# One block of a matrix product transposed by DMA instead of on TensorE, its first group reordered, and its block loads split in two and chained

## Chip, core and metric

The kernel runs on one core of one Trainium2 chip. The metric is the device time of one execution in microseconds; the figure for the kernel before is the median of three runs. Engines are called by their names: TensorE (PE in the views; PEld is its weight load), VectorE (DVE), ScalarE (ACT), GpSimd (POOL) and SyncE (SP). GpSimd issues the loads here, SyncE the stores and the DMA transposes.

## What is computed

```python
m, k, n = 2048, 2048, 2048          # a: m x k, b: k x n, gamma: n, all float32
x = np.matmul(a, b)
rms = np.sqrt(np.mean(x ** 2, axis=-1, keepdims=True) + eps)
return (gamma * x / rms).astype(np.float32)
```

## The kernel before, in words

**Blocks, groups, halves.** `a` is cut into 16 blocks of 128 rows (blocks 0 to 15), the output columns into two halves of 1024 (j = 0, 1), each half into two chunks of 512. Two blocks make a group g (blocks 2g and 2g + 1). The kernel keeps all of `b` in SBUF as bf16 (`raw`), loaded once. A matmul takes a 128 x 128 piece of transposed `a` as weights and a 128 x 512 piece of `b` as the moving operand and sums into one of eight PSUM banks: `tbank` and `acc[0]` to `acc[6]`.

**Head (blocks 0 to 3).** While `b` arrives, blocks 0 to 3 are multiplied plainly for the left half, and blocks 0 and 1 for the right half (`head_matmul`, L456, called by `stream_right`, L526). From there on every pair of blocks is multiplied for each half by seven products instead of eight (Strassen's scheme in Winograd's form): four quarters of `a` (2 blocks by even and odd pieces of k) and four of `b`. `product_matmul` (L359) issues one of the 8 matmuls of one of the products 1 to 7. Products 1, 2 take quarters of block 2g, 4 takes a quarter of block 2g + 1, and 5, 6, 7, 3 take sums of quarters, sum 1, 2, 3 and 4, which VectorE computes in `a_sums` (L337) from both transposed blocks. `PAIR` is group 1 (blocks 2 and 3), whose right half is done in this form while the head ends: banks `u2` = `acc[4]`, `u4` = `acc[5]`, `p7` = `acc[6]`. Its four chunks are `x11`, `x12`, `x21`, `x22`, and `plain` names the four chunks of blocks 0 and 1 on the right.

**Groups 2 to 7.** `halves` numbers the remaining (group, half) pairs: n = 0 is group 2 left, n = 1 group 2 right, n = 2 group 3 left, and so on. `do(n, m)` (L624) issues product m of half n and the copy by ScalarE that must follow it: after product 1, bank b1 is copied to bank b2; products 2 and 6 then go on summing in b1 and b2; after 6, b2 is copied to b3, where 5 and 3 go on summing; 4 goes on in b2; 7 has its own bank `B7` = `acc[2]`. Banks of an even n are b1 `acc[1]`, b2 `acc[3]`, b3 `acc[6]`; of an odd n `acc[0]`, `acc[4]`, `acc[5]`. `take(n, 11/12/22/21)` (L643) brings a result chunk from its bank to its place in SBUF (ScalarE copies 11 and 12, VectorE adds 22 and 21). So a product waits for the copy or add that frees or fills its bank, and for the sum or transposed block that is its weight operand.

**Preparing a block.** `load_block(mb)` (L135) loads 128 x 2048 float32, 1 MB, in one transfer that GpSimd issues; block 8 goes into the free end of `head_at`, others take turns in two buffers. `row_norm(mb)` (L226, ScalarE, two squares of 1024 columns and a root), `row_factor` (L236) and a scaling to fp16 (VectorE) follow. Then the block is transposed. Block 4 and block 5 are transposed on TensorE: `row_apply` (L247) scales the whole block, `transpose_half` (L197) issues 8 transposes per half of the block into a PSUM bank, `take_transposed` (L207) copies the bank to `at(mb)`. From block 6 on `prepare` (L251) does it: each half is scaled, and SyncE issues a DMA transpose of that half into `at(mb)`. `wait_for(src)` (L148) makes GpSimd copy one element of `src`, so that GpSimd's next load waits until `src` is there.

**Finishing rows.** `square_half`, `take_pre`, `square_right` (L282 to L306) make a row's rms on ScalarE with small sums on VectorE; `finish(mb, order)` (L313) multiplies each half of a block by 1/rms and gamma on VectorE, and SyncE stores it. The halves of x live in eight SBUF slots which are used again: half 0's chunks of block 4 take the slot of block 0's left half once that is stored.

**Order.** The schedule is written by hand: each engine runs its instructions in the order in which the program issues them, and waits at each for its operands. The part at issue is the code between the head and `first_segment` (L566 to L613), `first_segment` (L659, half 0) and `segment` (L689, halves 1 and on). Before the change its order on TensorE is: PAIR's product 7's end, product 6, product 3, product 5; block 4's 16 transposes; six matmuls of PAIR's product 4, block 5's first 8 transposes, the last two of product 4, block 5's other 8 (`turn`, L596); then do(0,1), do(0,7), do(0,2), do(0,6), do(1,1), do(0,5), do(0,4), do(1,6), do(0,3), do(1,2), do(2,1) and on. Blocks 6, 7 and 8 are loaded as soon as their buffers are free.

Of the kernel before, what the change touches and what calls it, by code (L numbers as in the profile page):

```python
# [17 lines left out]
def kernel(  # L18
# [13 lines left out]
    nc = tc.nc  # L32
    P = 128
# [101 lines left out]
    def load_block(mb):  # L135
        if mb == HB + 4:
            a32[mb] = head_flat[:, 2 * K:].bitcast(FP32)
        else:
            a32[mb] = a_pool.tile([P, K], FP32, name="a32")
        nc.gpsimd.dma_start(out=a32[mb], in_=a[mb * P:(mb + 1) * P, :])  # L140

    def load_gamma(j):
        half = slice(j * HALF, (j + 1) * HALF)
# [380 lines left out]
    def stream_right(kp):  # L524
        first, second = ([(g, 2 * kp + t) for g in plain] for t in range(2))
        if kp == 0:  # L526
            for both in zip(first, second):
                for g, kt in both:
                    head_matmul(banks[g], *g, kt)
            product_matmul(PAIR, 1, 1, u2, kp, True)  # L530
            product_matmul(PAIR, 1, 2, u4, kp, True)
            return
        product_matmul(PAIR, 1, 1, u2, kp, True)
        for g, kt in first:
            head_matmul(banks[g], *g, kt)
        if kp == KP - 1:
            product_matmul(PAIR, 1, 7, p7, kp - 1, True)
        product_matmul(PAIR, 1, 2, u4, kp, True)
        if kp < KP - 1:
            product_matmul(PAIR, 1, 7, p7, kp - 1, True)  # L540
        for g, kt in second:
            head_matmul(banks[g], *g, kt)

    for kp in range(KP):
        load_later(1)
        b_diff(1, kp)
# [17 lines left out]

    r2, r3 = HB - 2, HB - 1
    x11, x12, x21, x22 = (x_chunk(r, c) for r in (r2, r3) for c in (2, 3))
    copy_on("A")(out=x11, in_=u2)
    product_matmul(PAIR, 1, 7, p7, KP - 1, True)  # L570
    b_rest(1, KP - 1)
    add(x11, u4, x11)
    evict(plain[:1], "A")
    row_norm(HB)
    row_norm(HB + 1)
    product(PAIR, 1, 6, u2, start=False)
    nc.vector.tensor_copy(out=u4, in_=u2)
    row_factor(HB)
    row_apply(HB)
    evict(plain[1:2], "D")  # L580
    row_factor(HB + 1)
    row_apply(HB + 1)
    evict(plain[2:3], "A")
    product(PAIR, 1, 3, acc[0])
    product(PAIR, 1, 5, u4, start=False)
    turned = [transpose_half(HB, h, (tbank, acc[1])[h]) for h in range(2)]
    take_transposed(HB, 0, turned[0], nc.scalar.copy)
    take_transposed(HB, 1, turned[1], nc.vector.tensor_copy)
    load_block(HB + 3)
    for r in range(HB):  # L590
        take_pre(r)
    square_right(0)
    evict(plain[3:], "A")
    square_right(1)

    def turn(h):  # L596
        view = transpose_half(HB + 1, h, (tbank, acc[2])[h])
        take_transposed(HB + 1, h, view, nc.vector.tensor_copy)

    for kp in range(KP):  # L600
        if kp == 6:
            turn(0)
        product_matmul(PAIR, 1, 4, u2, kp, False)
    turn(1)
    load_block(HB + 4)
    a_sums(G0, (3, 1, 2), False)

    def pair_ends():
        nc.scalar.copy(out=x22, in_=p7)
        nc.scalar.copy(out=x12, in_=u4)  # L610
        add(x21, u2, x22)
        add(x22, x12, x22)
        add(x12, acc[0], x12)  # L613

    halves = [(g, j) for g in range(G0, NG) for j in range(2)]
    B1, B2, B3, B7 = (acc[1], acc[0]), acc[3:5], (acc[6], acc[5]), acc[2]

    def chunks(n):  # L620
        g, j = halves[n]
# [2 lines left out]
    def do(n, m, copies=True):  # L624
# [1 line left out]
        if n >= len(halves) or n < 0:  # L626
            return
        g, j = halves[n]
        b1, b2, b3 = B1[n % 2], B2[n % 2], B3[n % 2]
# [13 lines left out]
    def take(n, what, engine="A"):  # L643

        x11, x12, x21, x22 = chunks(n)
        if what == 11:
            copy_on(engine)(out=x11, in_=B1[n % 2])
# [11 lines left out]
    def first_segment():  # L659
        n, g, j = 0, G0, 0  # L660
        nxt = 2 * g + 2
        do(n, 1)
        do(n, 7, False)
        finish(0, (1,))
        pair_ends()
        do(n, 2)
        row_norm(nxt)
        a_sums(g, (4,))
        finish(0, (0,))
        do(n, 6)  # L670
        do(n + 1, 1)
        prepare(nxt)
        do(n, 5)
        nc.scalar.copy(out=chunks(n)[2], in_=B7)
        take(n, 22)
        row_norm(nxt + 1)
        take(n, 11)
        finish(1)
        do(n, 4)
        take(n, 21)  # L680
        prepare(nxt + 1)
        square_half(2 * g + 1, j)

    X2, W2, Y2 = tbank, B1[1], B1[0]
# [5 lines left out]
    def segment(n):  # L690
# [4 lines left out]
            block_segment(n)  # L695
            return
        first = g >= G2 and (g - G2) % 2 == 0
        do(n, 6)
        own = nxt + (g == NG - 2)
        if j == 0:  # L700
            finish(ra - 1)
# [10 lines left out]
        else:  # L712
# [316 lines left out]
```

## Time and profile before

| what | value |
|---|---|
| median of 3 runs | 218.91 us (218.74 to 219.53) |
| profiled execution, its own time | 218.44 us |
| its span, first to last instruction | 216.7 us |
| mean granted TensorE clock | 0.995 |
| TensorE busy | 206.6 us (95%), 996 matmuls and transposes |
| VectorE / ScalarE / GpSimd busy | 169.3 (78%) / 114.4 (53%) / 34.5 us (16%) |
| DMA | 46.60 MB, mean 215 GB/s |
| loads of blocks 6, 7, 8 issued at | 63.29, 66.17, 66.94 us |
| ... and landed after | 5.1, 6.1, 8.0 us |
| a DMA transpose of half a block, issue to landing | 3.0 / 3.3 / 5.7 us (least, median, most) |
| a store of half a block of rows, the first four | 2.6 / 2.8 / 4.8 us |

The profiled execution is one execution, and all durations of single instructions come from it. A timeline line has its start and length in us, engine, line of the kernel, operation and tiles; an instruction may start before the one ahead of it on its engine has quite ended, since they are pipelined. Matmuls follow one another every 0.216 us, while each is drawn 0.38 us long. A line of waits has the waiting engine, its tile and line, whom it waited for, and the total, the count and the longest.

### The profile page before, as it was taken

To read this page: it belongs to the slowest core of one execution; us is meant where nothing else is said; L and a number is where in the kernel's file an instruction comes from. 1 tells how busy PE (TensorE), PEld (TensorE's weight loads), DVE (VectorE), ACT (ScalarE), POOL (GpSimd) and SP (SyncE) were. 2 spreads that over 40 slices of the span, in tenths; PEclk is the share of its full clock that TensorE was granted. 3 is DMA by queue.
4 is the path that set the end of the run, shared out by engine and by line. 5 is a ranking of instruction groups with operands and counts; after the bars stand their busy time and mean duration, and the time that the engine had idled before them with its cause. 6 is when DMAs were issued, how large, how long until landed. Compare 5 with 4: busy or idle time off the path is not lost.

```text
span 216.7 us, 2965 instructions
## 1 busy us (share of the span) xinstructions
PE 206.6 (95%) x996; PEld 96.8 (45%) x1016; DVE 169.3 (78%) x336; ACT 114.4 (53%) x226; POOL 34.5 (16%) x73
## 2 busy tenths in 40 slices
PE   7999999999999999999999999999999999999960
PEld 3544544444455444444444444444444444444420
DVE  1127869999999997789875899479868999587981
ACT  2110001810499579499635972495686834556661
POOL 7554444433001000100021001101010000000010
PEclk9999999999999999999999999999999999999998
DMA  6999999999959788988574985588995971031446
GB/s 149 168 203 206 203 204 210 209 211 210 399 213 366 306 241 239 288 327 238 180 225 162 360 265 97 194 221 266 262 297 178 287 144 58 39 122 72 197 135 252
DMA packets 37040, 46.60 MB, mean 215 GB/s; under 512 B 22561, under 2 KB 26657, under 8 KB 35745
## 3 DMA queue, kind: packets, MB, share of 16 engines
q0 software_dynamic: 10608, 23.86, 45.0%
q1 hardware_dynamic: 26144, 22.29, 34.1%
q10 hardware_dynamic: 272, 0.26, 0.3%
q8 instruction: 8, 0.13, 0.2%
q14 instruction: 8, 0.06, 0.1%
HBM read 34.60 MB, written 16.78 MB: 237 GB/s over the span
## 4 chain that ended last, share of the span: by engine, by line
PE 91%; DMA 3%; issue 1%; ACT 1%; POOL 1%; DVE 0%; ACTq 0%; POOLq 0%
PE acc L367 63%; PE acc L457 16%; DMA early<-in_a_dram 3%; PE acc L406 3%; PE acc L448 2%; PE tbank L406 2%; PE tbank L486 2%; PE tbank L188 2%; ACT a L873 1%; POOL b L118 0%; PE acc L201 0%; PE tbank L201 0%; DVE head_at L193 0%; PE tbank L448 0%; ACT sq L981 0%
## 5 line engine op out<-in xcount | busy, mean ns | idle before, releaser
L457 PE MATMUL acc<-b,head_at 128*128 128x512 bf16 x171 | 42.1, 379 | 0.3
L279 ACT ACTIVATE sq<-x 128x1024 bf16<-128x1024 f32 (+1 forms) x31 | 31.5, 1016 | 20.2 <-DVE x L104 15.6
L367 PEld LDWEIGHTS <-s 128*128 128x128 f16 (+1 forms) x280 | 27.4, 98 | 33.1 <-DVE s L344 0.3
L318 DVE SCALAR_TENSOR_TENSOR x<-x,r,gamma_sb 128x1024 f32<-128x1024 f32 x28 | 35.0, 1282 | 0.5
L367 PE MATMUL acc<-b,head_at 128*128 128x512 bf16 x134 | 33.7, 379 | 0.3
L104 DVE TENSOR_TENSOR x<-acc,x 128x512 f32<-128x512 f32 x34 | 22.7, 687 | 10.4 <-PE acc L367 4.5
L367 PEld LDWEIGHTS <-head_at 128*128 128x128 f16 (+1 forms) x192 | 18.7, 98 | 22.2
L367 PE MATMUL acc<-b,at_even 128*128 128x512 bf16 x110 | 26.0, 379 | 0.1
L457 PEld LDWEIGHTS <-head_at 128*128 128x128 bf16 x176 | 16.9, 98 | 19.4 <-issue 0.4
L230 ACT ACTIVATE sq<-a 128x1024 bf16<-128x1024 f32 x22 | 23.3, 1058 | 2.1 <-DMA a<-in_a_dram 1.7
L367 PE MATMUL acc<-b,s 128*128 128x512 bf16 x103 | 24.2, 379 | 0.1
L367 PEld LDWEIGHTS <-at_even 128*128 128x128 f16 x160 | 15.6, 98 | 18.6
L367 PE MATMUL acc<-early,s 128*128 128x512 bf16 x93 | 23.5, 379 | 0.2
L118 POOL DMA_DIRECT2D b<-in_b_dram x32 | 17.2, 541 | 19.5 <-DMA b<-in_b_dram 13.0
L367 PE MATMUL acc<-t_left,s 128*128 128x512 bf16 x77 | 18.4, 379 | 0.1
L496 ACT COPY x<-acc 128x512 f32<-128x512 f32 x7 | 4.0, 581 | 25.3 <-PE acc L457 25.3
L639 ACT COPY acc<-acc 128x512 f32<-128x512 f32 x12 | 6.9, 574 | 8.0 <-PE acc L367 7.8
L193 DVE COPY head_at<-tbank 128x1024 bf16<-128x1024 bf16 x7 | 4.8, 692 | 7.7 <-PE tbank L188 7.7
L104 DVE TENSOR_TENSOR x<-tbank,x 128x512 f32<-128x512 f32 x9 | 6.2, 691 | 4.2 <-PE tbank L486 4.1
L876 POOL TENSOR_SCALAR x<-x,r 128x512 f32<-128x512 f32 x1 | 0.7, 697 | 48.1 <-DVE r L300 48.1
L367 PE MATMUL acc<-early,head_at 128*128 128x512 bf16 x32 | 7.7, 379 | 0.1
L104 DVE TENSOR_TENSOR early<-b 128x512 bf16<-128x512 bf16 x16 | 6.8, 422 | 0.6 <-DMA b<-in_b_dram 0.3
(157 smaller groups left out, 255.3 us busy)
## 6 DMA issues: line engine op xcount, KB each, us to landing
out_dram<-x SPq DMA_DIRECT2D x29, 512.0 KB, 3.0
a<-in_a_dram POOLq DMA_DIRECT2D x9, 1024.0 KB, 6.1
b<-in_b_dram POOLq DMA_DIRECT2D x32, 256.0 KB, 10.0
a<-in_a_dram POOLq DMA_DIRECT2D x4, 512.0 KB, 9.8
early<-in_a_dram POOLq DMA_DIRECT2D x7, 256.0 KB, 10.0
gamma_sb<-in_gamma_dram POOLq DMA_DIRECT2D x2, 512.0 KB, 9.9
head_at<-in_a_dram POOLq DMA_DIRECT2D x1, 1024.0 KB, 8.0
out_dram<-x SPq DMA_DIRECT2D x3, 256.0 KB, 2.6
```

Source lines behind the costliest of these rows:

```text
L104: nc.vector.tensor_tensor(out=out, in0=in0, in1=in1, op=op)
L118: nc.gpsimd.dma_start(out=raw[j][kp][:, t, :], in_=b[lo:lo + P, j * HALF:(j + 1) * HALF])
L188: nc.tensor.matmul(view[:, t, r, :], ah(kp)[:, r, t * P:(t + 1) * P], identity, is_transpose=True, start=(t == 0 and r == 0), stop=(t == 1 ...
L193: nc.vector.tensor_copy(out=head_at[:, 2 * kp:2 * kp + 2, :, :], in_=view)
L230: nc.scalar.activation(out=junk, in_=a32[mb][:, h * HALF:(h + 1) * HALF], func=ACTF.Square, scale=2.0 ** -8, accum_out=n2[:, h:h + 1])
L279: nc.scalar.activation(out=sq[:, 0:src.shape[-1]], in_=src, func=ACTF.Square, scale=inv_sqrt_n, accum_out=msq[mb][:, c:c + 1])
L318: nc.vector.scalar_tensor_tensor(out=x, in0=x, scalar=inverse_of[mb], in1=gamma_sb[:, h * HALF:(h + 1) * HALF], op0=ALU.mult, op1=ALU.mult)
L367: nc.tensor.matmul(bank, lhsT[:, kp, :], rhs, start=(start and kp == 0), stop=(kp == KP - 1), skip_group_check=not start)
L406: nc.tensor.matmul(bank, lhsT[:, k, :], rhs, start=(m in (1, 7) and k == 0), stop=(k == KQ - 1), skip_group_check=m not in (1, 7))
L448: nc.tensor.matmul(bank, lhsT[:, k, :], rhs[:, k, :], start=(m in (1, 7) and k == 0), stop=(k == KQ - 1), skip_group_check=m not in (1, 7))
L457: nc.tensor.matmul(bank, head_at[:, kt, r, :], head_rhs(c, kt), start=(kt == 0), stop=(kt == KT - 1))
L639: nc.scalar.copy(out=b3, in_=b2)
```

## The change

- Block 5 is scaled in two halves into `a16_first`, and SyncE transposes each by DMA; `turn` and its 16 TensorE transposes and two evictions are gone.
- Around it the order of the first group changes. x11's copy and the first four matmuls of PAIR's product 6 move ahead of the head's last four matmuls. PAIR's product 3 is cut into 4 + 2 + 2 matmuls and its product 4 into 6 + 2, and these lie between product 5, block 4's transposes and the products of group 2. Half 1's products 1 and 2 and its 6 move forward: do(0,1), do(1,1), do(0,2), do(1,2), the end of product 3, do(0,7), do(0,6), product 6 of half 1, do(0,5), do(0,4), do(0,3), do(2,1). Half 1's products 1 and 2 sum in `tbank` instead of `acc[0]`.
- `prepare(6)` now stands directly behind do(0,7), ahead of `finish(0, (0,))`; `finish(1)` is cut in two; `square_right(0)` and `square_right(1)` come behind do(0,1) and do(1,1).
- `load_block` issues two transfers of 1024 columns each. Block 7's load waits until block 6 is there (its last column), block 8's until block 7 is there; the wait in `segment` goes by the last column too.

```diff
@@ load_block
-        nc.gpsimd.dma_start(out=a32[mb], in_=a[mb * P:(mb + 1) * P, :])
+        for h in range(2):
+            half = slice(h * HALF, (h + 1) * HALF)
+            nc.gpsimd.dma_start(out=a32[mb][:, half], in_=a[mb * P:(mb + 1) * P, half])
@@ stream_right
         if kp == KP - 1:
+            copy_on("A")(out=x11, in_=u2)
             product_matmul(PAIR, 1, 7, p7, kp - 1, True)
+            for k in range(4):
+                product_matmul(PAIR, 1, 6, u2, k, False)
@@ between head and first_segment
-    product(PAIR, 1, 6, u2, start=False)
+    for kp in range(4, KP):
+        product_matmul(PAIR, 1, 6, u2, kp, False)
     nc.vector.tensor_copy(out=u4, in_=u2)
     row_factor(HB)
     row_apply(HB)
     evict(plain[1:2], "D")
     row_factor(HB + 1)
-    row_apply(HB + 1)
-    evict(plain[2:3], "A")
-    product(PAIR, 1, 3, acc[0])
-    product(PAIR, 1, 5, u4, start=False)
+    def part(m, bank, lo, hi, start=False):
+        for kp in range(lo, hi):
+            product_matmul(PAIR, 1, m, bank, kp, start)
+    part(3, acc[0], 0, 4, True)
+    part(5, u4, 0, KP)
+    part(4, u2, 0, 6)
     turned = [transpose_half(HB, h, (tbank, acc[1])[h]) for h in range(2)]
     take_transposed(HB, 0, turned[0], nc.scalar.copy)
     take_transposed(HB, 1, turned[1], nc.vector.tensor_copy)
+    src, f = a32.pop(HB + 1), factor.pop(HB + 1)
+    for h in range(2):
+        half = slice(h * HALF, (h + 1) * HALF)
+        nc.vector.tensor_scalar_mul(out=a16_first[:, half], in0=src[:, half], scalar1=f)
+        nc.sync.dma_start_transpose(at(HB + 1)[:, h * KP:(h + 1) * KP, :], a16_first[:, half])
+    wait_for(a32[HB + 2][:, K - 1:K])
     load_block(HB + 3)
     for r in range(HB):
         take_pre(r)
-    square_right(0)
-    evict(plain[3:], "A")
-    square_right(1)
...
-    load_block(HB + 4)
-    a_sums(G0, (3, 1, 2), False)
...
+    part(4, u2, 6, KP)
+    part(3, acc[0], 4, 6, True)
+    nc.scalar.copy(out=x21, in_=p7)
+    nc.scalar.copy(out=x12, in_=u4)
+    evict(plain[3:], "A")
+    add(x22, x12, x21)
+    add(x21, u2, x21)
+    evict(plain[2:3], "D")
+    x12_pair = x12
+    def b1_of(n):
+        return tbank if n == 1 else B1[n % 2]
@@ first_segment
         do(n, 1)
+        square_right(0)
+        do(n + 1, 1)
+        square_right(1)
+        do(n, 2)
+        do(n + 1, 2)
+        part(3, acc[0], 6, KP, True)
+        finish(0, (1,))
+        a_sums(g, (3, 1, 2), False)
         do(n, 7, False)
-        finish(0, (1,))
-        pair_ends()
-        do(n, 2)
         row_norm(nxt)
-        a_sums(g, (4,))
+        prepare(nxt)
+        add(x12_pair, acc[0], x12_pair)
         finish(0, (0,))
         do(n, 6)
-        do(n + 1, 1)
-        prepare(nxt)
+        load_after(a32[HB + 3][:, K - 1:K], HB + 4)
+        product(g, 1, 6, B2[1], False)
         do(n, 5)
         nc.scalar.copy(out=chunks(n)[2], in_=B7)
+        finish(1, (0,))
+        a_sums(g, (4,))
         take(n, 22)
         row_norm(nxt + 1)
+        nc.scalar.copy(out=B3[1], in_=B2[1])
         take(n, 11)
-        finish(1)
+        prepare(nxt + 1)
         do(n, 4)
         take(n, 21)
-        prepare(nxt + 1)
+        finish(1, (1,))
         square_half(2 * g + 1, j)
@@ segment
-        do(n, 6)
+        if n > 1:
+            do(n, 6)
...
-        if g < G2:
+        if g < G2 and n > 1:
             do(n, 2)
             take(n, 11)
...
         do(n + 1, 1)
+        if n == 1:
+            take(n, 11)
...
-                wait_for(a32[nxt + 2][:, 0:1])
+                wait_for(a32[nxt + 2][:, K - 1:K])
```

More of the change, by code (lines that the diff above doesn't have):

```diff
@@ L542, in stream_right @@
             head_matmul(banks[g], *g, kt)
+    r2, r3 = HB - 2, HB - 1
+    x11, x12, x21, x22 = (x_chunk(r, c) for r in (r2, r3) for c in (2, 3))
     for kp in range(KP):
@@ L563 @@
     load_block(HB + 2)
-    r2, r3 = HB - 2, HB - 1
-    x11, x12, x21, x22 = (x_chunk(r, c) for r in (r2, r3) for c in (2, 3))
-    copy_on("A")(out=x11, in_=u2)
     product_matmul(PAIR, 1, 7, p7, KP - 1, True)
@@ L591 @@
         take_pre(r)
-    square_right(0)
+    part(4, u2, 6, KP)
+    part(3, acc[0], 4, 6, True)
+    nc.scalar.copy(out=x21, in_=p7)
+    nc.scalar.copy(out=x12, in_=u4)
     evict(plain[3:], "A")
-    square_right(1)
[L596 to L604, printed above, removed]
-    load_block(HB + 4)
-    a_sums(G0, (3, 1, 2), False)
[L608 to L613, printed above, removed]
+    add(x22, x12, x21)
+    add(x21, u2, x21)
+    evict(plain[2:3], "D")
+    x12_pair = x12
     halves = [(g, j) for g in range(G0, NG) for j in range(2)]
     B1, B2, B3, B7 = (acc[1], acc[0]), acc[3:5], (acc[6], acc[5]), acc[2]
+    def b1_of(n):
+        return tbank if n == 1 else B1[n % 2]
     def chunks(n):
@@ L628, in do @@
         g, j = halves[n]
-        b1, b2, b3 = B1[n % 2], B2[n % 2], B3[n % 2]
+        b1, b2, b3 = b1_of(n), B2[n % 2], B3[n % 2]
         if g >= G2:
@@ L646, in take @@
         if what == 11:
-            copy_on(engine)(out=x11, in_=B1[n % 2])
+            copy_on(engine)(out=x11, in_=b1_of(n))
         elif what == 12:
```

## The prediction, made before the changed kernel was run

> **What bounds the kernel.** I read the page first (shares and slices), then TensorE's waits, then the chain, then each engine's timeline from 55 to 120 us, the stretch that the change touches. The page has TensorE busy 95%, with every slice but the first and the last two full. A table of busy time by stage (us, then TensorE, weight loads, VectorE, ScalarE, GpSimd, clock, DMA share, GB/s) says the same of our stretch:
>
> ```profile
> 57.00:66.00 9.00, 8.95 (x60) 4.76 (x60) 8.55 (x24) 7.98 (x15) 0.53 (x1) 1.00 0.73 281
> 66.00:75.00 9.00, 8.95 (x51) 4.36 (x50) 8.44 (x15) 6.96 (x16) 1.06 (x2) 1.00 0.91 367
> 75.00:84.00 9.00, 8.95 (x43) 4.05 (x43) 8.17 (x18) 6.60 (x13) 0.00 (x0) 1.00 0.75 236
> ```
>
> TensorE does not pause, at full granted clock, while VectorE is at 91 to 95%: a second engine is almost full. TensorE's own waits are two, both in the first 12 us:
>
> ```profile
> PE acc L167 <- DVE pace L158: 1.5, 1, 1.5
> PE tbank L486 <- DVE head_at L193: 0.3, 1, 0.3
> ```
>
> So from 12 to 209 us the time is the sum of TensorE's instructions. What the change can save is TensorE work; what it can cost is a pause of TensorE. The chain (start, us, what) shows the transposes of blocks 4 and 5:
>
> ```profile
> 63.57 0.45 PE tbank L201 x8
> 64.02 0.45 PE acc L201 x8
> 64.47 1.29 PE acc L367 x6
> 65.76 0.45 PE tbank L201 x8
> 66.21 0.43 PE acc L367 x2
> 66.64 0.45 PE acc L201 x8
> ```
>
> **What goes.** Block 5's two groups of 8 transposes (65.76 and 66.64) stand in the chain with 0.45 us each: 2 x 0.45 = 0.90 us go. Nothing else leaves TensorE; every product keeps its 8 matmuls of 0.216 us (1.73 us). 0.90 us is the ceiling. VectorE loses two evictions (L208, 0.69 each) and gains one (acc[2], 0.68, from ScalarE).
>
> **What it adds, by waits.** I set each engine's instructions in the new order, from 56 to 118 us, each starting when its engine and its inputs are free, with the durations of the rows (eviction 0.57 ScalarE, 0.68 VectorE; square of a half with its readout 1.18; row_norm 2.57; row_factor 0.70; scaling a half 0.75; finish of a half 1.28; 0.04 from one engine to the next). The old order set in this way gives do(2,6) at 91.11 where the trace has 91.10, and block 7's first scaling at 82.01 where it has 82.03. The new order gives, in old clock:
>
> - x11's copy ends 56.65 as before; the moved first four matmuls of product 6, which overwrite its bank, start 56.94: 0.25 us spare. They push the last head matmuls back 4 x 0.216 = 0.86 us, so the eviction of plain[0], both row norms and block 4's scaling come 0.86 later (scaling ends 63.59). Its transposes start at 63.92 (0.28 spare); the second bank is copied out by 64.19, wanted 64.37 (0.13 spare).
> - Product 5 needs u4, VectorE's copy of 60.16 to 60.86. Eight matmuls of product 3 lay beside it; now four, ending 60.82. **Pause 0.07.**
> - do(0,1) needs block 4's second half, copied 65.02 to 65.70; the matmuls before it end 65.68. **Pause 0.06.**
> - Block 5 is scaled in halves at 65.62 and 66.40, so SP issues its two DMA transposes at 66.4 and 67.8. They replace nothing on SP before finish(0)'s store at 71.2, and land 3.3 and 3.2 us after issue in quiet rows: 71.1. The first left operand made from it (sum 3) then ends 71.84, and do(0,7) wants it at 73.07. do(0,1), do(1,1), do(0,2), do(1,2) and the end of product 3, 7.3 us, are the cover: **no pause** until the landing passes 72.3, then 1:1.
> - VectorE is then full from 74.1 (prepare(6), the pair's x12, two finishes, sum 4) to do(0,5)'s end, and goes on through prepare(7), do(0,4)'s add, finish(1), ScalarE's two squares, finish(2) and the sums of group 3. The second ends at 90.37 and do(2,6) wants it at 90.33. **Pause 0.08.** In the old order do(2,6) had 2.2 us to spare there. ScalarE's copy for it ends 89.97 (0.4 spare).
> - take(0,11) waits for the store of block 0's left half, issued 78.4 instead of 75.3, since finish(0,(0,)) now stands behind prepare(6). Behind it on ScalarE stand only the squares, which wait for VectorE until 83.7. At a landing of 2.9 us the copy ends 81.9 and do(2,1) wants its bank at 83.43. Stores land 2.6 to 4.8 us after issue in these rows; at 4.8 do(2,1) pauses 0.39 but do(2,6) no longer does. I take 3.9 (block 8's load runs beside it): none.
> - GpSimd's added waits hold only loads: block 7 behind block 6's landing, block 8 behind block 7's. Nobody else needs GpSimd until the wait at 87.5. ScalarE starts row_norm(7) at 77.7 and needs the first half then, the second at 78.9. Block 6: buffer free 63.6, issue about 64.1, landing after 5.0 to 6.3 plus 0 to 0.7 for a second issue (two in a row stand 1.25 apart in the gamma rows, 0.53 at least): 69.1 to 71.1; wanted 71.4 and 72.6. Block 7: 0.6 for the wait and its issue, then the same: 74.7 to 78.1, I take 76.5. Spare: about 2 us. Block 8 follows by 84, wanted 94.3.
> - Later groups: the second transfer lets GpSimd's next load go up to 0.7 us later, but ScalarE can begin with the first half. Sums there end over 2 us ahead of their products (for group 6 at 160.2, wanted 162.8). I cost the split at nothing; uncovered, it would cost 0.7 at most per pair.
>
> Pauses: 0.07 + 0.06 + 0.08 = 0.21. Sum: -0.90 + 0.21 = **-0.7 us**. From group 4 on, do(4,6) starts at 114.58 instead of 115.28 and nothing closes up again. Against the profiled execution's 218.44 (span 216.7 and 1.7 around it) that is 217.74. This execution is 0.47 below the median 218.91 of the runs shown, so by that median: **218.2**.
>
> **Rivals.** *First: the transposes queue behind the load.* Block 6's load is still arriving when SP issues block 5's transposes. Here a load was issued at 150.14 and landed at 156.44 (6.3 us):
>
> ```profile
> 151.75 1.24 SPq L256 DMA_TRANSPOSE at_even<-a_half  x1
> 153.15 3.15 SPq L256 DMA_TRANSPOSE at_even<-a  x1
> ```
>
> They landed 5.7 and 5.2 us after issue, and the second blocked SP for 3.15 us. At 5.2 block 5 is there at 73.0: do(0,7) pauses 0.70, and the late sums push do(2,6) to 0.27. With 0.13 before, 1.1: net +0.2, 219.1. At 72.5 it is -0.3, 218.6. Against it: that load stood behind 0.5 MB of stores and had 3 us more to run; here the engines are empty at 64, and DMA rows show a lone 1 MB moved between 64.6 and 68.2.
>
> There is a rule that makes this one likelier. The Trainium skill, "SBUF — State Buffer", in "SBUF: two separate sides", says that GpSimd cannot write a load's descriptors while VectorE runs certain fast instructions out of SBUF, of the kind of these scalings, and that the load then waits. By it, block 6's second transfer, if it comes after 65.6, is held until the scalings end at 67.15 and lands near 71, and block 5's transposes near 73: 219.1 again. The trace cannot decide it: no load of the old kernel is issued inside a scaling, and in the head the issues keep their 1.25 us beat with VectorE idle (20 to 36 us) and busy (40 to 54).
>
> *Second, on the other side: block 7 comes late, and the kernel is slower than before.* The old kernel issued it at 66.17, over 10 us ahead of its norm; now it stands behind block 6's landing. From 78.3 (first half) or 79.2 (second) on, each us that it is late goes through row_norm(7), prepare(7), do(0,4)'s add, finish(2) and the sums into do(2,6), 1:1. The gain is used up from a second half at 80.0 on. The longest landings of a 1 MB load are 7.4 and 8.0 us; with block 6 at 71.1, 0.6, 8.0 and 0.7 it lands at 80.4, net +0.4, 219.3; one us more, by the stores and transposes that run beside it, 220.3. Against it: 8.0 was the last of three loads issued within 4 us, and now they are one at a time.
>
> *Third: VectorE takes over as the bound in the first group.* Its run from 74 to 90 has 0.4 us of slack in all; 3% on 16 us is 0.5 us, all paid at do(2,6): -0.2, 218.7. Against it: durations repeat within 0.01 us here.
>
> *Fourth: it does not save what it says.* The transposes would be free if TensorE waited behind them. The chain runs through all of them without a gap: 218.9 only if some pause of 0.9 stands there unseen.
>
> **Chances.** Forecast 0.61 (217.9 to 218.6, with the out-store pause inside); first rival 0.17; second 0.10; third 0.09; fourth 0.03. What a measurement of this kernel can tell from no change is about 0.5%, 1.09 us: more than the ceiling of 0.90, so a faster verdict needs scatter on top (the runs shown lie 0.8 apart): 0.12, out of the forecast. Slower needs over 2.0 us of pauses: most of the second rival and a little of the first, 0.12. The rest, 0.76, is within. The range: down to the ceiling (218.0) and 0.4 of scatter, 217.6; up through the first rival and the beginning of the second, 219.6.
>
> **What would show it.** TensorE without its 16 transposes (x980 matmuls instead of x996); in its waits no line in the middle, or lines of under 0.1 us for u4, block 4 and do(2,6). do(0,7) waiting for the DMA of block 5 is the first rival; do(2,6) waiting on a sum, with row_norm(7) waiting for its load, the second; the same with ScalarE on time, the third. Wrong altogether: a pause of over 0.3 us anywhere after 92 us, or TensorE's granted clock below 0.99.

## The result, and the profile after

The changed kernel takes 221.61 us (median of six runs, 220.08 to 222.58); the kernel before, on the same chip, 218.75 (218.67 to 219.53). The ratio is 1.0137, 95% interval 1.0112 to 1.0162: slower by 1.4%, and 2 us above the upper end of the forecast's range. Ratios, here and below, leave out executions that are over 1.5% longer than the fastest of the same kernel, so a ratio can differ from the quotient of the medians. The profiled execution is one of 221.46 us, span 219.7, mean granted clock 0.993.

The table by stage of the changed kernel, in the columns of the one shown of before, with a later row, and that row of before under it:

```profile
66.00:75.00 9.00, 8.50 (x40) 3.64 (x39) 6.57 (x14) 7.45 (x16) 1.24 (x3) 1.00 1.00 229
75.00:84.00 9.00, 9.00 (x43) 4.08 (x42) 8.69 (x20) 4.16 (x8) 1.49 (x3) 1.00 1.08 256
84.00:93.00 9.00, 7.72 (x36) 3.26 (x35) 5.98 (x8) 7.66 (x15) 1.69 (x3) 1.00 1.07 323
```

```profile
84.00:93.00 9.00, 8.95 (x42) 4.09 (x42) 7.13 (x12) 5.98 (x14) 0.72 (x2) 1.00 0.95 273
```

TensorE (first busy figure) now stops between 66 and 75 and between 84 and 93. Look at the last two columns too: the DMA engines are busier than before (1.00 and 1.08 against 0.91 and 0.75), but in 66 to 75 they move less (229 GB/s against 367). (The view counts a packet with its whole length where it starts, so a share can pass 1.) More of their time goes into small packets.

The chain of waits of the changed kernel, from block 4's transposes to group 3 and once more in group 5 (start, us, what); before, this stretch was TensorE's alone:

```profile
64.21 0.45 PE tbank L203 x8
64.66 0.45 PE acc L203 x8
...
67.92 5.11 DMA at_even<-a_first
...
73.13 0.70 DVE s L346
...
73.88 5.37 PE acc L369 x24
79.25 0.70 SPq L258
...
80.00 4.75 DMA out_dram<-x
...
84.82 0.06 ACT x L652
84.88 6.30 DMA head_at<-a
...
91.28 0.70 DVE head_at L346
...
92.01 0.70 DVE s L346
...
92.75 40.03 PE acc L369 x184
```

Only two groups of eight transposes are left: the 0.90 us did go. But transfers now stand in the chain: on the page they are 12% of it (before 3%, all of that the loads of the head). Three of them are in the first group. First, block 5's second DMA transpose takes 5.11 us, and do(0,7) waits behind sum 3. Second, block 0's left store takes 4.75 us, and ScalarE's copy take(0,11), which writes that slot, and do(2,1), which needs the bank, wait. Third, block 7's second transpose takes 6.30 us, and do(2,6) waits behind the sums. A fourth, of block 11 (3.50 us from 133.46), holds product 6 of half 6, do(6,6), in group 5; the expectations below call that product do(4,6).

TensorE's starts against the end of the matmuls ahead give the pauses: 0.17 at product 5, 0.08 at do(0,1), 0.66 at do(0,7) (73.88), 1.21 at do(2,1) (85.46), 0.38 at do(2,6) (92.75), 0.12 at do(6,1) (130.87) and 0.81 at do(6,6) (138.60). These are 3.43; less 0.90, and with 0.04 from the head, that is 2.57, and the trace has TensorE 2.61 us later (138.60 against 135.99). The other 0.4 us of the span come behind TensorE's last product. SyncE's timeline of the changed kernel shows the second cause beside the landings:

```profile
66.52 4.45 SPq L602 DMA_TRANSPOSE at_even<-a_first  x2
...
76.71 1.25 SPq L258 DMA_TRANSPOSE head_at<-a_half  x1
78.06 1.88 SPq L258 DMA_TRANSPOSE head_at<-a  x1
80.00 1.05 SPq L323 DMA_DIRECT2D out_dram<-x  x2
83.23 1.48 SPq L258 DMA_TRANSPOSE head_at<-a_half  x1
84.88 4.23 SPq L258 DMA_TRANSPOSE head_at<-a  x1
```

Before, the second transposes of blocks 6 and 7 were issued in 1.27 and 1.25 us:

```profile
78.17 1.27 SPq L256 DMA_TRANSPOSE head_at<-a  x1
84.27 1.25 SPq L256 DMA_TRANSPOSE head_at<-a  x1
```

They take 1.88 and 4.23 now, and the stores stand behind them. GpSimd's timeline has the loads, and the idle time in brackets at each COPY says how long it waited for a load:

```profile
64.17 1.05 POOL L142 DMA_DIRECT2D a<-in_a_dram  x2 [9.34 <-ACT norm L235]
71.43 0.18 POOL L151 COPY pace<-a 128x1 f32<-128x1 f32 x1 [6.20 <-DMA a<-in_a_dram]
72.02 1.05 POOL L142 DMA_DIRECT2D a<-in_a_dram  x2 [0.40 <-ACT rms L297]
80.22 0.44 POOL L151 COPY pace<-a 128x1 f32<-128x1 f32 x1 [7.15 <-DMA a<-in_a_dram]
80.68 1.05 POOL L142 DMA_DIRECT2D head_at<-in_a_dram  x2
```

Before, the three loads went out at 63.29, 66.17 and 66.94 and were all in by 75, so block 6's transposes (76.74, 3.3 and 3.1 us to land) had no load beside them. In the changed kernel block 6's load lies over block 5's transposes (5.7 and 5.1 us to land). Block 7's load, chained, lies over block 6's transposes (5.0 and 4.4), and block 8's over block 0's left store (4.7) and block 7's transposes (7.0 and 6.3). All of these land late.

### The profile page after: what moved, and what is told of

It reads as the page before. It is cut to its first block, busy times and chain, and to the rows that moved or that the text cites. A ratio compares the mean times of both kernels' runs of the same rounds, so it can differ in the third digit from the quotient of the medians.

```text
span 219.7 us, 2988 instructions
## 1 busy us (share of the span) xinstructions
PE 207.1 (94%) x1000; PEld 94.8 (43%) x1000; DVE 168.5 (77%) x336; ACT 113.9 (52%) x225; POOL 41.5 (19%) x85
## 4 chain that ended last, share of the span: by engine, by line
PE 79%; DMA 12%; DVE 2%; issue 1%; ACT 1%; POOL 1%; SPq 1%; DVEq 0%; ACTq 0%; POOLq 0%
PE acc L369 52%; PE acc L459 16%; DMA head_at<-a 4%; DMA early<-in_a_dram 3%; PE acc L408 3%; PE acc L450 2%; PE tbank L408 2%; DMA at_even<-a_first 2%; DMA out_dram<-x 2%; PE tbank L488 2%; PE tbank L190 2%; DVE s L346 1%; DVE head_at L346 1%; SPq L258 1%; ACT a L890 1%
## 5 line engine op out<-in xcount | busy, mean ns | idle before, releaser
L459 PE MATMUL acc<-b,head_at 128*128 128x512 bf16 x176 | 43.0, 379 | 0.8 <-DMA b<-in_b_dram 0.8
L281 ACT ACTIVATE sq<-x 128x1024 bf16<-128x1024 f32 (+1 forms) x31 | 31.5, 1016 | 18.6 <-DVE x L104 13.9
L369 PE MATMUL acc<-b,head_at 128*128 128x512 bf16 x136 | 33.8, 379 | 1.1 <-ACT x L652 1.0
L369 PE MATMUL acc<-b,s 128*128 128x512 bf16 x104 | 24.7, 379 | 0.0
L369 PE MATMUL acc<-b,at_even 128*128 128x512 bf16 x96 | 22.5, 379 | 0.0
L498 ACT COPY x<-acc 128x512 f32<-128x512 f32 x6 | 3.4, 592 | 26.1 <-PE acc L459 26.1
L644 ACT COPY acc<-acc 128x512 f32<-128x512 f32 x11 | 6.3, 574 | 10.9 <-PE acc L369 10.8
L142 POOL DMA_DIRECT2D a<-in_a_dram x18 | 9.5, 531 | 11.0 <-ACT norm L235 9.3
L151 POOL CAST pace<-at_even 128x1 f32<-128x1 f16 x3 | 1.6, 533 | 36.7 <-DMA at_even<-a 36.7
```

The source lines that it names most:

```text
L142: nc.gpsimd.dma_start(out=a32[mb][:, half], in_=a[mb * P:(mb + 1) * P, half])
L281: nc.scalar.activation(out=sq[:, 0:src.shape[-1]], in_=src, func=ACTF.Square, scale=inv_sqrt_n, accum_out=msq[mb][:, c:c + 1])
L369: nc.tensor.matmul(bank, lhsT[:, kp, :], rhs, start=(start and kp == 0), stop=(kp == KP - 1), skip_group_check=not start)
L459: nc.tensor.matmul(bank, head_at[:, kt, r, :], head_rhs(c, kt), start=(kt == 0), stop=(kt == KT - 1))
L644: nc.scalar.copy(out=b3, in_=b2)
```

## The experiments

Theory A: loads, DMA transposes and stores share the 16 DMA engines; the chain puts each load onto transfers that are wanted soon, and TensorE waits for these. Its rivals were that the split, the chain by itself, or an order that is too tight costs the time. All runs are compared with the kernel before on the same chip (medians 218.2 to 218.43). From here on a pause is the idle time that the timeline gives unless the text says "by starts"; that view draws a matmul 0.38 us long, so it comes out 0.16 less. In this measure the changed kernel pauses 0.50 at do(0,7), 1.05 at do(2,1), 0.23 at do(2,6) and 0.65 at do(6,6).

**1. one_transfer**: the changed kernel with `load_block` in one transfer again.

```diff
-        for h in range(2):
-            half = slice(h * HALF, (h + 1) * HALF)
-            nc.gpsimd.dma_start(out=a32[mb][:, half], in_=a[mb * P:(mb + 1) * P, half])
+        nc.gpsimd.dma_start(out=a32[mb], in_=a[mb * P:(mb + 1) * P, :])
```

> The changed kernel with each of blocks 6 to 15 loaded by one transfer of 2048 columns again; order, waits and DMA transposes stay. Theory A (the DMA engines are the bound of the first group: loads, DMA transposes and stores are moved onto one another, and the split makes each load land later and so makes more of these collisions): the pause of 1.0 us before do(4,6) goes, block 6 lands near 69.5 instead of 71.4, do(0,7)'s pause falls from 0.66 to 0 to 0.3, and the pauses at do(2,1) and do(2,6), 1.6 together, fall to under 0.8: 219.0 to 220.3. Theory B (the new order on VectorE and ScalarE is too tight by itself): only the pause before do(4,6) can go, 220.5 to 221.5. Theory C (the split alone is to blame): all pauses but 0.25 go, 218.2 to 218.8.

223.82 us, from 219.03 to 225.83, too scattered for a ratio: five executions lie at 222.4 or above, and the one of 219.03 has no trace. In five of six executions undoing the split does not give the time back; theory C's forecast is missed, and theory A's too. The profiled execution (223.64) has no pause at do(0,7) and none at do(6,6); its one pause is 3.88 us at do(2,1), where ScalarE's copy waits for block 0's left store:

```profile
ACT x L650 <- DMA out_dram<-x: 5.8, 1, 5.8
```

That store went out at 78.82 and landed 7.8 us later, beside block 8's load of 78.32. The pause is paid twice: after it TensorE's granted clock falls. The stages of that execution:

```profile
80.00:84.00 4.00, 3.40 (x15) 1.47 (x15) 3.86 (x10) 0.87 (x3) 0.00 (x0) 1.00 0.88 225
84.00:90.00 6.00, 2.67 (x7) 1.01 (x7) 0.92 (x2) 3.25 (x7) 0.03 (x1) 0.78 1.10 351
```

The clock (third figure from the end) is 0.78 in 84 to 90, and the eight matmuls of do(2,1) take 3.53 us, in other rows 1.89. By stages of 2 us the clock is 0.85, 0.50 and 0.80 from 86 to 92, which is 2 x (0.15 + 0.50 + 0.20) = 1.7 us lost on top of the 3.88.

**2. store_early**: the changed kernel with block 0's left half finished and stored together with its right half, ahead of group 2's sums.

```diff
-        finish(0, (1,))
+        finish(0, (1, 0))
...
-        finish(0, (0,))
```

> The changed kernel with block 0's left half finished together with its right half, ahead of group 2's sums, where VectorE waited 1.8 us for block 5; so its store is issued near 73 instead of 80. Theory A: do(2,1)'s pause of 1.21 goes, but block 7's transposed rows, which land at 91.2, hold do(2,6) as before, so the pause moves there: 221.2 to 221.7. Theory B (tight order): the wait of take(0,11) was one of its links, 1.2 us go: 220.2 to 220.6.

222.99 us, 1.0185 (1.0155 to 1.0214). do(2,1) falls from 1.05 to 0.27 and do(0,7) from 0.50 to 0.17, but do(2,6) rises from 0.23 to 2.06: with a store more beside it, block 7's load, issued at 71.66, lands at 81.7, and ScalarE's norm waits 2.4 us for it. Behind that pause the granted clock falls as well, to 0.50 in 94 to 96 and 0.66 in 96 to 98 us: 2 x (0.50 + 0.34) = 1.7 us again, so this kernel's 1.85% is pauses and clock. One collision removed makes the next.

**3. unchained**: the changed kernel without the two waits on GpSimd ahead of the loads of blocks 7 and 8.

```diff
-    wait_for(a32[HB + 2][:, K - 1:K])
     load_block(HB + 3)
...
-        load_after(a32[HB + 3][:, K - 1:K], HB + 4)
+        load_block(HB + 4)
```

> The changed kernel without the two added waits of GpSimd: blocks 7 and 8 are loaded as soon as their place is free. Theory A: 2 MB more stand beside block 5's DMA transposes, which land at 74 to 76 instead of 73.0, so do(0,7) pauses 1.5 to 3.5 us, while the pauses at do(2,1) and do(2,6) shrink because loads 7 and 8 are over by 78: 221 to 223. Rival (the chained loads are the cause, and transposes do not suffer from loads beside them): do(0,7)'s pause stays at 0.66 and the later two go, 219.5 to 220.2.

229.03 us, 1.0447 (1.0413 to 1.0481). TensorE's waits in it:

```profile
PE acc L369 <- DVE s L346: 10.1, 2, 9.5
```

Block 5's second transpose, issued at 68.0, lands 14.1 us later, behind four half loads issued from 67.8 to 69.4. So the chain is there for a reason: without it the loads starve the transposes. The profiled execution is one of 231.5, the fastest 227.65; theory A had the place and the sign, with 1.5 to 3.5 us for the pause. In it, from 77 to 87 us, during the pause of 9.48 us and behind it, the granted clock is 0.50.

**4. turn_back**: the changed kernel with block 5 transposed on TensorE, behind do(0,1).

```diff
-        nc.sync.dma_start_transpose(at(HB + 1)[:, h * KP:(h + 1) * KP, :], a16_first[:, half])
+    a16[HB + 1] = a16_first
...
+        turned = [transpose_half(HB + 1, h, (acc[6], acc[5])[h]) for h in range(2)]
+        for h in range(2):
+            take_transposed(HB + 1, h, turned[h], nc.vector.tensor_copy)
```

The transposes go into banks over which products 3 and 5 of group 2 go on summing, so those sums come out changed; the instructions are the same in kind and number.

> The changed kernel with block 5 transposed on TensorE again: its 16 transposes stand behind do(0,1), into acc[6] and acc[5], which are free there, and VectorE copies both out; everything else stays as changed. TensorE has 0.90 us more to do. Theory A: do(0,7) does not pause, block 6 lands by 69.8, blocks 7 and 8 follow earlier, the pauses at do(2,1) and do(2,6) fall to 0 to 0.6 together, the one before do(4,6) may stay (up to 1.0): 219.2 to 220.4. Theory B (tight order on VectorE, which has 1.4 us more here): 221.8 to 222.8.

224.47 us, 1.0279 (1.0242 to 1.0317), with 222.12 for the profiled execution. Without the two DMA transposes block 6 lands at 69.5 (71.4 in the changed kernel) and block 7 at 76.4 (80.1), and do(0,7) and do(2,6) do not pause; the clock stays at 1.00. But block 8's load then goes out at 76.95 and lies on block 0's left store, issued at 78.88: do(2,1) pauses 3.59. Theory B's range has the 222.12, but this pause waits for a store and not for VectorE. Theory A's collisions are shown, its sum for this kernel was not: I had not followed block 8's load to its new place.

**5. before_split**: the kernel before with the loads in two transfers alone.

```diff
-        nc.gpsimd.dma_start(out=a32[mb], in_=a[mb * P:(mb + 1) * P, :])
+        for h in range(2):
+            half = slice(h * HALF, (h + 1) * HALF)
+            nc.gpsimd.dma_start(out=a32[mb][:, half], in_=a[mb * P:(mb + 1) * P, half])
...
-                wait_for(a32[nxt + 2][:, 0:1])
+                wait_for(a32[nxt + 2][:, K - 1:K])
```

> The kernel before with nothing changed but the split: blocks 6 to 15 in two transfers of 1024 columns, the wait by the last column. Theory A (collisions on the DMA engines, which the moved work brings about; the split only makes loads land some tenths later): in the old order loads 6 to 8 are over before block 6's DMA transposes start, so the split costs little, 0 to +0.4 against before. Theory C (the split is the main cost): +1 us or more.

218.70 us, 1.0027 (1.0009 to 1.0046): the split costs 0.6 us by the ratio in the old order, with no pause of TensorE in the middle; where it goes the profile does not show.

**6 to 8. one_store, one_store_late8, late8**: both repairs together (single transfers as in 1, early stores as in 2); the same with block 8's load moved behind block 7's transposes; and the changed kernel with that move alone.

```diff
-        load_after(a32[HB + 3][:, K - 1:K], HB + 4)
...
+            if g == G0:
+                load_block(HB + 4)
```

> The changed kernel with both undone: one transfer for each block, and block 0's left half finished and stored ahead of group 2's sums. Theory A: do(2,1) no longer waits for that store; block 8's load still stands on block 7's DMA transposes, so those land late and do(2,6) pauses 0.5 to 2: 218.7 to 220.3. Rival (the store was the only late thing): no pause over 0.3, 217.7 to 218.1.

> one_store, and block 8's load behind block 7's DMA transposes (it goes out with the wait that stands ahead of block 9's load) instead of behind block 7's load. Theory A: no load stands on block 7's transposes or on the stores any more, all pauses together are under 0.5, and the 0.90 us of TensorE work shows: 217.6 to 218.1, below the kernel before. Rival (DMA transposes of block 5 cost as much as they save, whatever stands beside them): 218.4 or more.

> The changed kernel with block 8's load alone moved behind block 7's DMA transposes; two transfers each, the store late as changed. Theory A: block 0's store and block 7's transposes have only each other beside them, do(2,1) pauses 0 to 0.4, do(2,6) 0 to 0.5, do(0,7)'s 0.66 stays and the one before do(4,6) may: 218.8 to 220.2. Rival (block 8's load is not what delays the store, SP's own queue is): do(2,1) pauses 1 us or more, 220.5 to 222.

| kernel | median us | ratio (95%) | pauses in its profile, us |
|---|---|---|---|
| one_store | 220.30 | 1.0104 (1.0070 to 1.0138) | do(0,7) 0.30, do(2,6) 1.41 |
| one_store_late8 | 221.56 | 1.0159 (1.0132 to 1.0186) | do(0,7) 0.38, do(2,1) 0.62, do(2,6) 1.54, do(6,1) 0.84, do(6,6) 0.61 |
| late8 | 220.95 | 1.0112 (1.0089 to 1.0136) | do(0,7) 0.90, do(2,1) 0.29, do(6,1) 0.45, do(6,6) 1.32 |

In late8 nothing loads beside block 7's transposes: SyncE issues them in 1.24 and 1.25 us, not 1.48 and 4.23, they land after 3.4 and 3.2 us, and do(2,6) does not pause. So block 8's load was what held them. But group 5 then pauses longer (do(6,1) and do(6,6)); that the moved load does this is not shown. In one_store what is left is block 7's load, issued at 72.01 and in at 80.0. one_store_late8 missed theory A's forecast by 3.5 us: block 7's load still takes 8.7 us, and do(2,6) pauses as in one_store. Its rival, that block 5's DMA transposes cost as much as they save, is not refuted by any run.

**9 to 11. one_store_turn, one_store_turn_free, before_chained**: one_store with block 5 on TensorE; the same without the chain; and the kernel before with the chain alone.

```diff
+    def turn(h):
+        view = transpose_half(HB + 1, h, acc[2])
+        take_transposed(HB + 1, h, view, nc.vector.tensor_copy)
...
         do(n + 1, 1)
         square_right(1)
+        turn(0)
         do(n, 2)
+        finish(0, (1,))
+        turn(1)
```

The version without the chain leaves the two waits out, as in 3; before_chained adds them to the kernel before:

```diff
+    wait_for(a32[HB + 2][:, K - 1:K])
     load_block(HB + 3)
...
+    wait_for(a32[HB + 3][:, K - 1:K])
     load_block(HB + 4)
```

> The version with single transfers and both stores of block 0 early, but block 5 transposed on TensorE again: each group of 8 transposes into acc[2], one behind do(1,1), one behind do(0,2), evicted by VectorE. The chain of loads 6, 7 and 8 is kept. Theory A (loads, DMA transposes and stores collide on the 16 DMA engines): without block 5's transposes load 6 lands near 69.6 and load 7 near 76.5 (as where block 5 was turned back before), row_norm(7) no longer waits, block 7's transposes go before load 8 is half done, and do(2,6) pauses 0 to 0.5 instead of 1.41; do(2,1) no longer waits for a store. TensorE has 0.90 us more to do. 218.2 to 219.4. Rival B (the new order itself is too tight on VectorE and ScalarE, whatever moves by DMA): do(2,6) still pauses over 1 us, 220 or more.

> The same, with the chain taken away: the loads of blocks 7 and 8 wait for nothing but their buffers, as in the kernel before. Theory A: with no DMA transpose of block 5 beside them the three loads can starve nothing, as in the kernel before, whose loads were over by 75 us; loads land by 76, block 6's and 7's transposes run on quiet engines (3 to 4 us), no pause over 0.2 in the middle: 218.2 to 218.8, the lowest of the three. That the chain costs by itself would show as the distance to the version before. Rival B (order too tight): do(2,6) or do(2,1) still pauses over 0.5, 219.3 or more.

> The kernel before with the chain alone: block 7's load waits for block 6's last column, block 8's for block 7's. The old order, old transposes on TensorE, single transfers. Theory A: loads 7 and 8 now lie beside block 6's DMA transposes and block 0's store, so these land 1 to 2 us later than 3.3, but nothing of block 5 is there to push them; the old order has 2.2 us to spare at do(2,6): 0 to +0.6 on the kernel before, 218.3 to 219.0. Rival C (the chain alone makes the loss): +1 or more, 219.4 to 221.

| order | chain | median us | ratio (95%) |
|---|---|---|---|
| old (before_chained) | yes | 219.04 | 1.0028 (1.0012 to 1.0044) |
| new (one_store_turn_free) | no | 220.06 | 1.0071 (1.0052 to 1.0090) |
| new (one_store_turn) | yes | 221.86 | 1.0140 (1.0120 to 1.0160) |

The chain costs 0.3% in the old order and, with not one DMA transpose of block 5, 0.7% in the new one. Here theory A's forecast for one_store_turn was wrong, and rival B's numbers came out. The chain of waits has a transfer behind them; block 7's load was early, and yet:

```profile
78.49 7.49 DMA head_at<-a_half
...
86.08 0.77 DVE a_half L255
```

`prepare` scales the first half of every block into the same buffer, `a16_half`. Block 6's first transpose, with block 8's load (77.05) beside it, takes 7.49 us to read it out, and VectorE may not scale block 7 before that. That stops VectorE for 2.57 us, and do(2,6) pauses 1.90. The old order has the same late transposes. VectorE's waits in before_chained:

```profile
DVE head_at L344 <- DMA head_at<-a: 2.3, 2, 2.0
DVE a_half L255 <- DMA head_at<-a_half: 1.8, 2, 1.7
```

VectorE waits 3.7 us in the middle, and TensorE pauses 0.2: do(2,6) had 2.2 us to spare. Alone the chain costs 0.3% and the new order 0.7%; together they cost 1.4%.

**12 and 13. turn_own_half, free_own_half**: the two new-order kernels of 9 and 10, block 7's first half scaled into a buffer of its own (the one that held block 5).

```diff
-        for h, dst in enumerate((a16_half, src.bitcast(FP16)[:, 0:HALF])):
+        for h, dst in enumerate((a16_first[:, 0:HALF] if mb == HB + 3 else a16_half, src.bitcast(FP16)[:, 0:HALF])):
```

> The version with single transfers, both stores of block 0 early, block 5 on TensorE and the chain (one_store_turn), with one edit: block 7's first scaled half gets a buffer of its own (the one that held block 5), so VectorE need not wait until block 6's first DMA transpose has read the shared one. Theory A (the chain puts block 8's load on block 6's transposes; their late landing holds VectorE by the shared half buffer, and the new order has no slack for it): VectorE's wait of 2.57 us at 83.5 goes, do(2,6)'s pause of 1.9 falls to 0 to 0.8, do(2,1)'s 0.55 stays since it waits for the landing itself: 1.1 to 1.9 us less than one_store_turn, 219.9 to 220.8. Rival D (the shared buffer hides a limit of SyncE's or of the DMA engines behind it: block 7's transposes are not earlier, since SyncE is blocked until 84.8): do(2,6) still pauses over 1.2, 221.2 or more.

> The same edit in the version without the chain (one_store_turn_free), whose one profile has no pause over 0.3 and whose other executions were some 0.9 longer than that one. If those were late transposes that held VectorE by the shared half buffer in some executions, this is 0.3 to 0.9 us less: 219.1 to 219.7. If the new order itself takes that time (no slack on VectorE and ScalarE), it is the same: 219.9 to 220.2.

turn_own_half 219.42 us, 1.0047 (1.0031 to 1.0063); free_own_half 219.06, 1.0048 (1.0026 to 1.0071). One buffer takes 0.9% off the chained kernel, and with it the chain costs nothing that the times show; without the chain its gain of 0.2% is within the noise. SyncE's line in turn_own_half shows that it was the buffer and not SyncE, though SyncE was blocked as long:

```profile
77.42 2.05 SPq L256 DMA_TRANSPOSE head_at<-a_half  x1
79.58 4.07 SPq L256 DMA_TRANSPOSE head_at<-a  x1
...
84.37 1.63 SPq L256 DMA_TRANSPOSE head_at<-a_first  x1
```

Block 7's transposes go out at 84.37, with the shared buffer at 86.91, and do(2,6) waits for nothing. What stays is 0.5% in both. By starts the profiles have pauses at product 5 for u4 (0.29 in turn_own_half, 0.66 in free_own_half) and 0.08 to 0.14 at two or three later places, which are the new order's, and in turn_own_half 0.6 at do(2,1), which waits for block 6's first DMA transpose and so is still the chain's.

**14. one_store_own_half**: the same buffer in one_store, where block 5 is transposed by DMA and VectorE did not wait for the shared one.

> The same buffer of its own for block 7's first half, now in the version that keeps block 5's DMA transposes (one_store: single transfers, both stores of block 0 early, the chain). In one_store VectorE did not wait for the shared buffer: do(2,6)'s 1.41 came from block 7's load, issued at 72.01 beside block 5's last transpose and block 0's stores and landed at 80.1. Theory A: the edit changes nothing here, do(2,6) still pauses 1 to 2 us and waits on a row norm that waits for its load: 219.9 to 220.7. Rival E (the edit helps by something else than that wait, such as the place of the buffer): as much as on the version with TensorE's transposes, 2 us less than one_store: 218.0 to 218.8, which would also be the first version with the new order that is no slower than the kernel before.

220.57 us, 1.0099 (1.0081 to 1.0116), as one_store. The buffer helps only where its wait was. The chain of waits still has block 7's load in it:

```profile
72.11 8.67 DMA a<-in_a_dram
...
80.80 1.16 ACT sq L230 x2
```

With TensorE's transposes instead (turn_own_half) the same load was out at 69.78 and in by 75.0, 5.2 us. So the version with block 5's DMA transposes is the slower one by 0.5% (1.0099 against 1.0047), although TensorE has 0.90 us less to do. That the load goes out 2.3 us later is the transposes' doing: block 6's load, ahead of it, takes 6.9 us beside them and 5.1 without. Of the 3.4 us that it then takes longer this is not shown: block 0's left store goes out at 72.44 in one_store_own_half, beside the load, and at 76.02 in turn_own_half, and the two were not separated. No version was faster than the kernel before.

## Why the prediction was wrong, step by step

- **The 0.90 us that goes** was right: 16 transposes fewer, at 0.45 a group, in the chain. The count that was to show it, 980 matmuls, does not: the page has 1000, since 20 matmuls are missing in the trace of before (its 996 stand for 1016; a gap of one matmul stands in it every 10.8 us). The order on the engines was right where no transfer ends a wait: SyncE issues block 5's transposes at 66.52 and 67.92 (worked out 66.4 and 67.8), do(0,1) pauses 0.08 (0.06). u4's pause was 0.17 (0.07), and up to 0.66 in other kernels of the new order: a margin of some tenths in a plan is not a margin.
- **do(0,7), "no pause until the landing passes 72.3, then 1:1".** The point and the slope were right, the landing was not: 73.0 instead of 71.1, pause 0.66. That is the first rival, to the tenth (73.0, 0.70). Its reason is the DMA engines. What they served in 66 to 69 us and in 69 to 72 (packets, MB, share of 16 engines; q0 carries GpSimd's loads, q1 SyncE's transfers):

```profile
q0 software_dynamic: 249, 0.93, 94.5%
q1 hardware_dynamic: 91, 0.02, 3.4%
```

```profile
q1 hardware_dynamic: 1416, 0.35, 119.0%
q0 software_dynamic: 19, 0.04, 3.5%
```

  Block 6's load is served almost alone, then the transposes. The Trainium skill, "DMA: Bandwidth & Descriptors", in "Queues, rings and completion order", says that a DMA engine takes turns between its queues packet by packet. The trace agrees in part, if its packets are the page's: a load's packet is 3.7 KB here (0.93 MB in 249) and a transpose's 0.25 KB (0.35 MB in 1416), so with equal turns the transposes move one byte for fifteen of the load. All 91 packets of the transposes start after 68 us, and from 68 to 69 the load got 95: about equal turns. The longest stretch of it is in unchained, from 72 to 77 us:

```profile
q0 software_dynamic: 423, 1.55, 90.7%
q1 hardware_dynamic: 500, 0.13, 15.5%
```

  From 86 to 88 us of the changed kernel it is not so: block 8's load got 203 packets, SyncE's queue 3, and why is open. The Trainium skill's other rule ("SBUF — State Buffer", in "SBUF: two separate sides"), on VectorE's scalings holding a load, is not needed for block 6: both halves of its load were issued by 64.69, ahead of the scalings (65.75), and in turn_back, where the scalings stand at the same place (65.3), the load lands at 69.5.
- **do(2,1), "I take 3.9 … none".** It is the largest pause of the first group, 1.21. The landing was inside the rows that I had (4.7 of 2.6 to 4.8, priced at 0.39); the issue was not. I put the store at 78.4; it went out at 80.00. VectorE had finished that half at 79.22, late by its wait for block 5, and SyncE was blocked until 79.94 by block 6's second transpose.
- **"GpSimd's added waits hold only loads."** This is the step that failed. Their price was worked out as lateness of the loads; what the loads do in their new places to SyncE's transposes and issues beside them was left at nothing, and block 5's landing, beside block 6's load, was taken from quiet rows in the same way. In place of 0.08 us at these three products the trace has 0.66 + 1.21 + 0.38 = 2.25 of its 3.43 us, each behind a transfer that landed late beside a load. Block 7 itself was 3.6 us later than taken (80.1 against 76.5, outside 74.7 to 78.1), close to the second rival's 80.4. But in this profile do(2,6)'s 0.38 is not the late norm: it is block 7's transposes, 7.0 and 6.3 us to land beside block 8's load, which late8 showed. The second rival had the right sign and place for store_early and one_store, where the norm is what is late.
- **"VectorE's run from 74 to 90 has 0.4 us of slack in all"** was written down as a rival of 0.5 us by 3%. It is what makes the collisions cost: in the old order VectorE's 3.7 us of waits became 0.2 of TensorE, in the new one 2.57 became 1.90 (before_chained, one_store_turn). I counted the lost 2.2 us of slack at do(2,6) as a pause of 0.08, not as the loss of the cover for every late transfer ahead of it.
- **The split at nothing** was nearly right: 0.27% in the old order. That the pause "of over 0.3 us anywhere after 92 us" came at do(6,6) is in part open. Load 11 goes out at 119.55 (116.50 before), lies beside block 10's transposes of 124.02 and 126.10, and SyncE is blocked 1.91 and 3.55 us; VectorE waits 0.83 for the shared half buffer. But late8 and one_store_late8 pause there too and store_early, also split, does not, so the split alone is not it. A second half buffer for the later blocks was not tried.
- **Also open**: several kernels' other executions are longer than the profiled one (turn_back 222.12 against a median of 224.47, 2.4 more). The clock's fall, 1.7 us in two profiles, came after pauses of 3.88 and 2.06 us and not after turn_back's 3.59, so it may come in some executions of one kernel and not in others. The mean granted clocks fit that: 0.990 for turn_back's 222.12, 0.982 to 0.985 for four of its five longer executions, and a fall of 1.7 us is 0.008 of the span. Those executions have no trace, so where their clock fell is not shown.

## What to carry to other kernels

Before a load is moved or chained, list every DMA transpose and store in the stretch that it will then cover, and price their landings and their issues by rows taken under a load (here mostly 4.4 to 7.5 us for a transpose, not 3.3), together with each buffer that a transfer must finish reading before an engine may write it. An engine's slack ahead of a product is what pays for late transfers; an order that spends it makes costs that were hidden show, so test such an order with the slack counted in us of lateness per transfer. A transpose taken off the bounding engine is not free when its packets share the DMA engines with loads that are just in time: here the version that saves 0.90 us on TensorE was 1.1 us slower than its nearest partner, where a load went out 2.3 us later.

## What the runs showed of the hardware that was not expected

- A DMA transpose's issue blocks SyncE for 1.24 to 1.33 us in the first groups of the kernel before, with no load beside it, and for up to 4.3 us beside a load (one_store_turn); the stores behind it on SyncE wait as long.
- A transfer of SyncE beside GpSimd's loads lands late by far: a half block's transpose after 14.1 us in unchained (3.1 to 3.3 with no load beside it), a store after 7.8 us in one_transfer (2.8 at the median before).
- TensorE's granted clock can fall after a pause, to 0.50 for 3.4 us: after 3.88 us (one_transfer) and 2.06 (store_early), and during 9.48 (unchained, for 10.2 us); not after 3.59 (turn_back), nor after 1.90 or less. In the first two it costs 1.7 us more. The Trainium skill, "TensorE: Matmul & The Clock Gate", in "What's actually happening", gives half speed after an idle window of some 3.4 us that runs freely, whatever the kernel does. The 0.50 agrees, and so does it that the length of a pause alone does not decide; that 2.06 us were enough does not.
